# Loading eight channel tiles of x and of their weights singly instead of four, with the squares and the table product issued behind a later step

## The chip, the cores and the metric

The kernel runs on one core of a Trainium2 chip. The metric is the time of one execution on the device in microseconds (us), as the median of some runs. The engines named below are TensorE (PE, matmuls; PEld is its weight load), VectorE (DVE), ScalarE (ACT), GpSimd (POOL) and SyncE (SP, which here only issues DMAs).

## What is computed

One layer of a streaming encoder on 320 positions (256 of a prompt and 64 of a running stream), model width 2048, in float32. Cut to what matters:

```python
z = rmsnorm(x, ln_mix_g) @ w_in                # (320, 2048) @ (2048, 3328)
q, k, v, zs = split(z)                         # 1024, 128, 128, 2048 columns
bias = rel_bias_table[t5_bucket(q_pos - k_pos)]  # 16 heads, one table of 32 rows
a = sink_attention(rmsnorm(q), rmsnorm(k), v, bias, sinks)
s = u * (W_s @ rmsnorm(v_s) + b)               # u, v_s = halves of gelu(zs)
x = x + concat(rmsnorm(a), rmsnorm(s)) @ w_out
x = x + square(relu(rmsnorm(x) @ w_ffn_up)) @ w_ffn_down
```

## The kernel before

Everything is kept transposed: a tile has 128 channels on the partitions and the 320 positions along its rows. x is 16 such channel tiles (k = 0 to 15). A product runs over the channel tiles; for each block of weights of 256 output columns, PE adds up two banks of 128 columns. Float32 is brought to PE as two halves: the high half is the value rounded by an ACT copy (line 125 for weights, line 178 for x, where the gain is multiplied in), the low half is the rest, by DVE (lines 126 and 179). Three matmuls of 128x128 by 320 make one product: high by high, low x by high weight, high x by low weight (line 136).

The first product (`products` with `first=load_x`) is special: x itself is loaded in it, and two jobs go side by side, the k and v columns (tile `acc`) and the first 256 query columns (tile `q_ps`). `chunks` cuts the 16 channel tiles into steps: before, four steps of one tile and then three of four tiles. For each step `load_x` loads x and splits it, then for each of the two jobs the weights are loaded (`w_first`), split into `w_hi` and `w_lo` (three buffers each), and multiplied. So one tile brings 12 matmuls, and a step of four tiles 24 for each job. The norm of x is applied behind the product: squares of x (line 247, eight ACT instructions of two tiles each) are added up, and the reciprocal root is multiplied into the result.

The order of the instructions on each engine is laid out by a planner at build time, which takes the instruction that is ready first in its own reckoning, and among ready ones the one that comes earlier in the program. It can be held: `keep_in_program_order` puts an instruction behind the one before it on its engine in the program, which is done for the splits of the steps of one tile; `issue_after(ins)` puts what is in its block behind `ins` on the engine of `ins`. `steps` keeps, for each step and job, the ACT split, the DVE split and the last matmul: before, `steps[8]` and `steps[9]` are the two jobs of tiles 4 to 7.

The table product (line 228) multiplies the bias table by a one-hot matrix. Its result goes to `b_row` by a DVE copy (line 230), to `b_dram` in DRAM by a DMA of POOL (line 232), and from there by 16 loads into `bias`. These loads wait in the list `between`, and `load` (line 99) puts four of them behind each of the next loads of weights. All loads go out from SP in the one order in which `load` is called. The weights that come next, behind the first product, are those of the queries (`w_raw`, steps of four tiles).

Of the kernel before, what the change touches and what calls it, by code (L numbers as in the profile page):

```python
# [29 lines left out]
def hymba_step_kernel(ctx: ExitStack, tc: tile.TileContext, i, o):  # L30
# [13 lines left out]
    def misc():  # L44
        return ps_m.tile([P, 512], F32, name="misc", tag="misc")

    def big(name):
        return actp.tile([P, KT, T], F32R, name=name, tag="A", bufs=2)

    def blk(name, shape, dt=F32):  # L50
        return actp.tile(shape, dt, name=name, tag="B", bufs=6)
# [3 lines left out]
    xT = const.tile([P, KT, T], F32, name="xT")  # L55
    cols = const.tile([P, 58], F32, name="cols")
    g_mix, g_ffn = cols[:, 0:16], cols[:, 16:32]
# [34 lines left out]
    loads, between, steps = [], [], []  # L92

    def load(out, in_):


        for o_, i_ in [(out, in_)] + [between.pop(0) for _ in range(min(4, len(between)))]:
            with tc.issue_after(loads[-1].ins) if loads else nullcontext():
                loads.append(nc.sync.dma_start(out=o_, in_=i_))  # L99

    def chunks(n, first):
        if first:
            return [(a, 1) for a in range(4)] + [(a, 4) for a in range(4, n, 4)]
        return [(a, 4) for a in range(0, n, 4)]

    def products(w, k0, nk, jobs, rh, rl, first=None, deep=None):


        wv = w.rearrange("(kt p) n -> p kt n", p=P)
        steps.clear()  # L110
        for a, n in chunks(nk, first is not None):
            if first is not None:
                first(a, n)
                if a % 4 == 0:
                    ahead = blk("w_first", [P, len(jobs), 4, 256])
            for j, (c0, ps) in enumerate(jobs):
                if first is not None:
                    raw = ahead[:, j, a % 4:a % 4 + n]
                else:
                    raw = (deep or wp).tile([P, 4, 256], F32, name="w_raw", tag="w_raw")  # L120
                hi = wp.tile([P, 4, 256], F32R, name="w_hi", tag="w_hi", bufs=3)
                lo = wp.tile([P, 4, 256], F32R, name="w_lo", tag="w_lo", bufs=3)
                load(raw[:, :n], wv[:, k0 + a:k0 + a + n, c0:c0 + 256])
                pin = tc.keep_in_program_order if first is not None and a < 4 else lambda ins: ins
                high = pin(nc.scalar.activation(out=hi[:, :n], in_=raw[:, :n], func=AF.Copy))  # L125
                low = pin(nc.vector.tensor_tensor(out=lo[:, :n], in0=raw[:, :n], in1=hi[:, :n].bitcast(F32),  # L126
                                                  op=ALU.subtract))
                tail = isinstance(ps, list) and a + n == nk
                kgs = [(k, g) for g in range(2) for k in range(n)] if tail else [(k, g) for k in range(n) for g in range(2)]
                passes = [(w_, r_, x) for x, (w_, r_) in enumerate(((hi, rh), (hi, rl), (lo, rh)))]  # L130

                for (k, g), (w_, r_, x) in [(kg, p_) for p_ in passes for kg in kgs] if first is not None else \
                        [(kg, p_) for kg in kgs for p_ in passes]:
                    kk = a + k
                    out = ps[g][:, 0:T] if isinstance(ps, list) else ps[:, g, 0:T]
                    mm = nc.tensor.matmul(out=out, lhsT=w_[:, k, g * P:(g + 1) * P], rhs=r_(kk),  # L136
                                          start=(kk == 0 and x == 0), stop=(kk == nk - 1 and x == 2))
                steps.append((high.ins, low.ins, mm.ins))
# [10 lines left out]
    def product(w, k0, nk, c0, rh, rl, deep=None, apart=False):  # L149
        ps = [misc(), misc()] if apart else acc_tile()  # L150
        products(w, k0, nk, [(c0, ps)], rh, rl, deep=deep)
        return ps
# [22 lines left out]
    def split(src, g, hi, lo, pinned=False):  # L175

        pin = tc.keep_in_program_order if pinned else lambda ins: ins
        pin(nc.scalar.activation(out=hi, in_=src, func=AF.Copy, scale=g))  # L178
        pin(nc.vector.scalar_tensor_tensor(out=lo, in0=src, scalar=g, in1=hi.bitcast(F32), op0=ALU.mult,
                                           op1=ALU.subtract))  # L180


    XH, XL = big("XH"), big("XL")
    def load_x(a, n):
        load(xT[:, a:a + n], xv[:, a:a + n])
        for k in range(a, a + n):
            split(xT[:, k], g_mix[:, k:k + 1], XH[:, k], XL[:, k], pinned=a < 4)
    xh, xl = (lambda k: XH[:, k]), (lambda k: XL[:, k])
    w_in = i["w_in"]

# [3 lines left out]
    kv_ps = acc_tile()  # L194
    q0_ps = ps_sc.tile([P, 2, 512], F32, name="q0_ps", tag="s_ps")
    products(w_in, 0, KT, [(1024, kv_ps), (0, q0_ps)], xh, xl, first=load_x)

    kvx = blk("kvx", [P, 1152])
# [25 lines left out]


    b_ps = misc()
    with tc.issue_after(steps[9][2]):
        nc.tensor.matmul(out=b_ps[0:16, 0:255], lhsT=tab, rhs=oneh, start=True, stop=True)
    b_row = sm.tile([16, 255], F32, name="b_row", tag="w1", bufs=3)
    nc.vector.tensor_copy(out=b_row, in_=b_ps[0:16, 0:255])  # L230
# [12 lines left out]
    ssq2 = sm.tile([P, 2, T], F32, name="ssq2", tag="w2", bufs=4)  # L243
    for k in range(0, KT, 2):
        sq = sm.tile([P, 2, T], F32, name="sq2", tag="w2", bufs=4) if k else ssq2
        with tc.issue_after(steps[9][0]):
            nc.scalar.activation(out=sq, in_=xT[:, k:k + 2], func=AF.Square)
        if k:
            nc.vector.tensor_tensor(out=ssq2, in0=ssq2, in1=sq, op=ALU.add)
# [321 lines left out]
```

## Time and profile before

| | |
|---|---|
| median of 3 runs | 1263.6 us (1261.91 to 1265.82) |
| profiled execution | 1262.26 us |
| its span in the profile | 1259.7 us |
| PE busy | 1252.3 us, 8519 matmul records |
| DVE, ACT, POOL busy | 637.9, 489.4, 106.1 us |
| read from HBM | 182.91 MB |

The span is what the profile covers of one execution; the rest of the profiled execution's time lies around it. A timeline row gives the start, the busy time, engine, line, the tile written and those read, the shape, the count of merged instructions, and in brackets the idle time of the engine before it with what ended it. A matmul's record is longer than its share of the pace, since matmuls overlap. A row of an engine's queue (SPq) is the issue of a DMA, not its transfer.

### The profile page before, as it was taken

How to read it: one execution, taken by the hardware profiler on the slowest of the kernel's cores; microseconds unless marked ns; L12 is line 12 of the kernel's file. 1: busy time of each engine (PE TensorE's matmuls, PEld its weight loads, DVE VectorE, ACT ScalarE, POOL GpSimd, SP SyncE). 2: the span in 40 equal slices, each digit the busy share in tenths (PEclk: the TensorE clock that was granted, in tenths of full speed). 3: DMA queues.
4: the chain of work that ended last, by engine and by line, in shares of the span. 5: the costliest groups of instructions: out<-in, count | busy, mean ns of one | idle time of the engine just before them, and what ended most of it. 6: DMA issues, size and time to landing. Idle time of an engine off the chain costs nothing.

```text
span 1259.7 us, 20182 instructions
## 1 busy us (share of the span) xinstructions
PE 1252.3 (99%) x8519; PEld 1236.6 (98%) x8519; DVE 637.9 (51%) x731; ACT 489.4 (39%) x636; POOL 106.1 (8%) x104
## 2 busy tenths in 40 slices
PE   8999999999999999999999999999999999999998
PEld 7998889999999999999999999999999999999998
DVE  7547857756864444444444444444444334444443
ACT  7335546533543342223333333343333333343221
POOL 2213452400310000000000000000000000000000
PEclk9999999999999999999999999999999999999999
DMA  8643233644454444445544444455444444444550
GB/s 281 191 136 116 85 109 119 216 148 137 151 149 148 152 149 149 149 147 150 150 150 151 150 151 151 151 151 151 150 151 150 146 148 149 148 153 160 169 169 32
DMA packets 186426, 187.77 MB, mean 149 GB/s; under 512 B 6464, under 2 KB 185856, under 8 KB 186336
## 3 DMA queue, kind: packets, MB, share of 16 engines
q1 hardware_dynamic: 185696, 185.43, 47.2%
q8 instruction: 66, 1.08, 0.4%
q0 software_dynamic: 496, 1.03, 0.3%
q14 instruction: 24, 0.20, 0.0%
q10 hardware_dynamic: 144, 0.03, 0.0%
HBM read 182.91 MB, written 3.32 MB: 148 GB/s over the span
## 4 chain that ended last, share of the span: by engine, by line
PE 98%; DMA 0%; SPq 0%; ACT 0%; issue 0%; DVE 0%
PE acc L136 93%; PE misc L136 1%; PE q_ps L136 1%; PE s_ps L329 1%; PE misc L374 1%; PE misc L365 1%; DMA xT<-in_xT 0%; SPq L99 0%; PE misc L275 0%; PE misc L430 0%; PE misc L158 0%; PE misc L422 0%; PE misc L169 0%; ACT XH L178 0%; PE misc L431 0%; ACT w_hi L125 0%
## 5 line engine op out<-in xcount | busy, mean ns | idle before, releaser
L126 DVE TENSOR_TENSOR w_lo<-w_raw,w_hi 128x1024 fp32r<-128x1024 f32 x332 | 413.6, 1246 | 460.6 <-ACT w_hi L125 451.2
L125 ACT ACTIVATE w_hi<-w_raw 128x1024 fp32r<-128x1024 f32 x332 | 351.9, 1060 | 708.0 <-PE acc L136 674.6
L136 PE MATMUL acc<-H2H,w_hi 128*128 128x320 f32 x1024 | 316.6, 309 | 0.0
L136 PE MATMUL acc<-H2L,w_hi 128*128 128x320 f32 x1024 | 316.4, 309 | 0.0
L136 PE MATMUL acc<-H2H,w_lo 128*128 128x320 f32 x1024 | 316.4, 309 | 0.0
L136 PE MATMUL acc<-FH,w_hi 128*128 128x320 f32 x992 | 306.5, 309 | 0.0
L136 PE MATMUL acc<-FL,w_hi 128*128 128x320 f32 x992 | 306.5, 309 | 0.0
L136 PE MATMUL acc<-FH,w_lo 128*128 128x320 f32 x992 | 306.5, 309 | 0.0
L136 PEld LDWEIGHTS acc<-H2L,w_hi 128*128 128x128 f32 x1024 | 192.2, 188 | 0.0
L136 PEld LDWEIGHTS acc<-H2H,w_hi 128*128 128x128 f32 x1024 | 192.2, 188 | 0.0
L136 PEld LDWEIGHTS acc<-H2H,w_lo 128*128 128x128 f32 x1024 | 192.2, 188 | 0.0
L136 PEld LDWEIGHTS acc<-FH,w_hi 128*128 128x128 f32 x992 | 186.2, 188 | 0.0
L136 PEld LDWEIGHTS acc<-FL,w_hi 128*128 128x128 f32 x992 | 186.2, 188 | 0.0
L136 PEld LDWEIGHTS acc<-FH,w_lo 128*128 128x128 f32 x992 | 186.2, 188 | 0.0
L136 PE MATMUL acc<-XH,w_hi 128*128 128x320 f32 x384 | 117.2, 316 | 1.2 <-ACT w_hi L125 1.1
L136 PE MATMUL acc<-XH,w_lo 128*128 128x320 f32 x384 | 116.8, 315 | 0.0
L136 PE MATMUL acc<-XL,w_hi 128*128 128x320 f32 x384 | 116.6, 314 | 0.0
L136 PEld LDWEIGHTS acc<-XH,w_hi 128*128 128x128 f32 x384 | 71.2, 189 | 4.7 <-ACT w_hi L125 2.2
L136 PEld LDWEIGHTS acc<-XL,w_hi 128*128 128x128 f32 x384 | 71.4, 189 | 2.4 <-issue 1.9
L136 PEld LDWEIGHTS acc<-XH,w_lo 128*128 128x128 f32 x384 | 71.1, 188 | 2.2 <-issue 1.5
L488 DVE SCALAR_TENSOR_TENSOR tf<-acc,r 128x640 f32<-128x640 f32 x32 | 26.4, 825 | 42.7 <-PE acc L136 42.7
L502 DVE TENSOR_TENSOR xT<-xT,acc 128x640 f32<-128x640 f32 x31 | 25.5, 821 | 41.8 <-PE acc L136 41.8
(176 smaller groups left out, 1016.9 us busy)
## 6 DMA issues: line engine op xcount, KB each, us to landing
w_raw<-in_w_up SPq DMA_DIRECT2D x128, 512.0 KB
w_raw<-in_w_down SPq DMA_DIRECT2D x128, 512.0 KB
w_raw<-in_w_in SPq DMA_DIRECT2D x44, 512.0 KB
w_raw<-in_w_out SPq DMA_DIRECT2D x32, 512.0 KB
w_first<-in_w_in SPq DMA_DIRECT2D x6, 512.0 KB
out_yT<-xT SPq DMA_DIRECT2D x7, 320.0 KB
xT<-in_xT SPq DMA_DIRECT2D x3, 640.0 KB
w_first<-in_w_in SPq DMA_DIRECT2D x8, 128.0 KB
```

The costliest lines, as they stand in the source:

```text
L125: high = pin(nc.scalar.activation(out=hi[:, :n], in_=raw[:, :n], func=AF.Copy))
L126: low = pin(nc.vector.tensor_tensor(out=lo[:, :n], in0=raw[:, :n], in1=hi[:, :n].bitcast(F32), op=ALU.subtract))
L136: mm = nc.tensor.matmul(out=out, lhsT=w_[:, k, g * P:(g + 1) * P], rhs=r_(kk), start=(kk == 0 and x == 0), stop=(kk == nk - 1 and x == 2))
L329: nc.tensor.matmul(out=s_ps[:, j, 0:2 * nk].rearrange("x (p k) -> x p k", p=2), lhsT=qT[:, blk_, a:a + 2].rearrange("p a t -> p (a t)"), r ...
L365: nc.tensor.transpose(out=pt_ps[0:n, (2 * p + j) * P:(2 * p + j + 1) * P], in_=s[:, p, j, c:c + n], identity=ident)
L374: nc.tensor.matmul(out=o_ps[p * HD:(p + 1) * HD, 0:256], lhsT=v[0:n, kv], rhs=pt[0:n, p * 256:(p + 1) * 256], start=(x == 0), stop=(x == l ...
L488: nc.vector.scalar_tensor_tensor(out=t, in0=ps[:, :, 0:T], scalar=0.0, in1=r2[:, None, :].to_broadcast([P, 2, T]), op0=ALU.max, op1=ALU.mult)
L502: nc.vector.tensor_tensor(out=xT[:, a:a + n], in0=xT[:, a:a + n], in1=p, op=ALU.add)
```

## The change

In the first product the channel tiles 0 to 7, instead of 0 to 3, make steps of one tile each; tiles 8 to 15 stay two steps of four. The splits of x and of the weights are held in program order for all eight. With ten steps and two jobs, `steps` has 20 entries: 0 to 15 are the single tiles, 16 and 17 the two jobs of tiles 8 to 11. The table product now follows `steps[17]`, the last matmul of the second job of tiles 8 to 11; the squares follow `steps[11]`, the ACT split of the second job of tile 5.

```diff
     def chunks(n, first):
         if first:
-            return [(a, 1) for a in range(4)] + [(a, 4) for a in range(4, n, 4)]
+            return [(a, 1) for a in range(8)] + [(a, 4) for a in range(8, n, 4)]
...
-                pin = tc.keep_in_program_order if first is not None and a < 4 else lambda ins: ins
+                pin = tc.keep_in_program_order if first is not None and a < 8 else lambda ins: ins
...
-            split(xT[:, k], g_mix[:, k:k + 1], XH[:, k], XL[:, k], pinned=a < 4)
+            split(xT[:, k], g_mix[:, k:k + 1], XH[:, k], XL[:, k], pinned=a < 8)
...
-    with tc.issue_after(steps[9][2]):
+    with tc.issue_after(steps[17][2]):
         nc.tensor.matmul(out=b_ps[0:16, 0:255], lhsT=tab, rhs=oneh, start=True, stop=True)
...
-        with tc.issue_after(steps[9][0]):
+        with tc.issue_after(steps[11][0]):
             nc.scalar.activation(out=sq, in_=xT[:, k:k + 2], func=AF.Square)
```

## Rows read from the trace of the kernel before

**Rows 1.** From the page: the span, the first engine's busy time, the granted clock of PE in 40 slices, and the share of the engines in the chain that ended last.

```profile
span 1259.7 us, 20182 instructions
...
PE 1252.3 (99%) x8519; PEld 1236.6 (98%) x8519; DVE 637.9 (51%) x731; ACT 489.4 (39%) x636; POOL 106.1 (8%) x104
...
PEclk9999999999999999999999999999999999999999
...
PE 98%; DMA 0%; SPq 0%; ACT 0%; issue 0%; DVE 0%
```

**Rows 2.** All waits of PE in the whole span: who waited, for whom, us in total, how often, the longest.

```profile
PE q_ps L136 <- ACT w_hi L125: 1.5, 1, 1.5
PE misc L77 <- DVE hsel L87: 1.3, 1, 1.3
PE acc L136 <- ACT w_hi L125: 1.1, 1, 1.1
```

**Rows 3.** Two windows of the first product: the stretch, its length, the busy time of each engine in it, the granted clock, the busy share of the DMA engines and what they moved.

```profile
4.27:11.83 7.56, 7.50 (x42) 6.98 (x42) 4.53 (x11) 3.88 (x9) 2.97 (x7) 1.00 0.93 288
11.83:15.82 3.99, 1.33 (x9) 0.89 (x7) 2.30 (x6) 3.21 (x7) 0.00 (x0) 1.00 1.06 362
```

**Rows 4.** Timeline of PE over the first product.

```profile
13.51 0.56 PE L136 MATMUL q_ps<-XH,w_hi 128*128 128x320 f32 x2 [1.53 <-ACT w_hi L125]
...
15.82 1.44 PE L136 MATMUL acc<-XH,w_hi 128*128 128x320 f32 x8 [1.13 <-ACT w_hi L125]
...
23.05 0.60 PE L228 MATMUL misc<-oneh,tab 32*16 32x255 f32 x2
23.58 1.43 PE L136 MATMUL acc<-XH,w_hi 128*128 128x320 f32 x8
...
30.72 1.33 PE L136 MATMUL acc<-XH,w_hi 128*128 128x320 f32 x8
...
33.06 1.34 PE L136 MATMUL q_ps<-XH,w_hi 128*128 128x320 f32 x8
...
34.38 1.34 PE L136 MATMUL acc<-XH,w_lo 128*128 128x320 f32 x8
```

**Rows 5.** Timeline of ACT over the same stretch.

```profile
8.07 0.77 ACT L125 ACTIVATE w_hi<-w_first 128x256 fp32r<-128x256 f32 x2 [0.25 <-DMA w_first<-in_w_in]
...
12.59 0.56 ACT L178 ACTIVATE XH<-xT,cols 128x320 fp32r<-128x320 f32 x1 [2.91 <-DMA xT<-in_xT]
13.06 0.40 ACT L125 ACTIVATE w_hi<-w_first 128x256 fp32r<-128x256 f32 x1
...
14.73 2.12 ACT L125 ACTIVATE w_hi<-w_first 128x1024 fp32r<-128x1024 f32 x2
...
17.38 1.99 ACT L247 ACTIVATE sq<-xT 128x640 f32<-128x640 f32 x3
19.26 1.92 ACT L178 ACTIVATE XH<-xT,cols 128x320 fp32r<-128x320 f32 x4
```

**Rows 6.** Timeline of SP's queue: the issues of the loads.

```profile
3.56 0.43 SPq L99 DMA_DIRECT2D xT<-in_xT  x1
4.04 0.91 SPq L99 DMA_DIRECT2D w_first<-in_w_in  x2
...
6.41 0.43 SPq L99 DMA_DIRECT2D xT<-in_xT  x1
...
30.48 2.59 SPq L99 DMA_DIRECT2D bias<-b_dram  x4
33.12 0.44 SPq L99 DMA_DIRECT2D w_raw<-in_w_in  x1
```

**Rows 7.** Windows of 5 us (columns as in rows 3; the last one is GB/s).

```profile
0.00:5.00 5.00, 3.66 (x9) 2.58 (x10) 1.55 (x12) 2.35 (x4) 3.74 (x13) 1.00 0.55 141
5.00:10.00 5.00, 4.94 (x29) 4.54 (x29) 3.73 (x9) 3.88 (x9) 2.34 (x5) 1.00 0.90 272
10.00:15.00 5.00, 3.15 (x20) 2.61 (x18) 2.05 (x6) 2.41 (x6) 0.00 (x0) 1.00 1.03 345
```

**Rows 8.** The chain behind the table product: the copy and the DMA to DRAM in the timelines of DVE and POOL; and two lines of the list of DMA issues (KB of one, us from issue to landing).

```profile
24.31 0.40 DVE L230 COPY b_row<-misc 16x255 f32<-16x255 f32 x1
...
25.01 0.58 POOL L232 DMA_DIRECT2D b_dram<-b_row  x1 [17.52 <-DVE b_row L230]
...
b_dram<-b_row POOLq DMA_DIRECT2D x1, 239.1 KB, 5.5
...
out_kpT<-kvx POOLq DMA_DIRECT2D x1, 64.0 KB, 2.0
```

**Rows 9.** The second step (tiles 4 to 7) of the next product: its split on ACT and DVE, and its first matmul with the high half and its first with the low half in PE's timeline.

```profile
37.12 1.06 ACT L125 ACTIVATE w_hi<-w_raw 128x1024 fp32r<-128x1024 f32 x1 [5.33 <-DMA w_raw<-in_w_in]
...
38.21 1.23 DVE L126 TENSOR_TENSOR w_lo<-w_raw,w_hi 128x1024 fp32r<-128x1024 f32 x1 [4.50 <-ACT w_hi L125]
...
41.95 0.31 PE L136 MATMUL acc<-XH,w_hi 128*128 128x320 f32 x1
...
42.24 0.31 PE L136 MATMUL acc<-XH,w_lo 128*128 128x320 f32 x1
```

**Rows 10.** Two windows of 1 us, one of them while the table was written to DRAM (columns as in rows 3).

```profile
25.00:26.00 1.00, 1.00 (x9) 1.00 (x8) 1.00 (x2) 1.00 (x3) 0.58 (x1) 1.00 1.01 395
...
30.00:31.00 1.00, 1.00 (x9) 1.00 (x8) 1.00 (x3) 0.27 (x1) 0.00 (x0) 1.00 0.01 4
```

## The prediction

> **What bounds the kernel now.** I read the page first: TensorE (PE) is busy 1252.3 of 1259.7 us, its clock is granted in full in every slice, and the chain that ended last is PE for 98% [rows 1]. A microsecond in which PE stands still is therefore a microsecond of the result, and a microsecond saved on another engine is nothing unless PE was waiting for it. Next come PE's waits: there are three in the whole kernel, 1.5 and 1.1 us on line 136 for ACT's high half of the weights and 1.3 us before the warm-up [rows 2]. So all that can be won lies in the first 16 us. The windows by stage say where: from 4.27 to 11.83 PE is busy all but 0.06 us, from 11.83 to 15.82 only 1.33 us of 3.99 [rows 3]. The timeline shows what stood still: the second job of tile 3 starts at 13.51 instead of 11.83, and tiles 4 to 7 start at 15.82 [rows 4].
>
> ACT's timeline gives the reason [rows 5]. The high half for tile 3's second job (13.06) stands behind the split of x tile 4 (12.59), which waited 2.91 us for the transfer of x tiles 4 to 7, issued at 6.41 [rows 6]. Behind it come three more splits and the 1024-wide high half (14.73), and only then can PE go on. From 15.82 PE runs without a gap. Had it run on from 11.83 with tile 3's second job (12 matmuls of a tile go in 7.14/4 = 1.79 us, from the stretch 23.58 to 30.72 [rows 4], so half a tile is 0.89), tile 4 would have started at 12.72: the loss before tile 4 is 3.1 us, and that is the most that any cure of this gap can give.
>
> **Part 1: x and weights of tiles 4 to 7 one at a time.** PE work is unchanged (same matmuls, same order of tiles). Three transfers become twelve. SP issues a tile's three in 1.43 us (x at 3.56 for tile 2 and at 6.41 for tile 4, 2.85 for two tiles [rows 6]), so tile 7 is issued by 6.41 + 4 x 1.43 = 12.1 us; that is behind PE's back as long as the data come in time. A small transfer took 8.07 - 4.04 = 4.0 us from issue to use (tile 2's weights [rows 5, 6]); the 640 KB one took 12.59 - 6.41 = 6.2. With 4.5 for a small one in the loaded queue, tile 4 is there at 7.4 + 4.5 = 11.9 at the latest, then one tile each 1.43 us: 13.3, 14.7, 16.2. PE wants them at 12.72, 14.5, 16.3 and 18.1. ACT's part of a tile is one split and two 256-wide halves; by the pieces in a row (four splits 1.92 us, two such halves 0.77 [rows 5]) that is 0.48 + 0.77, 1.25 us, under PE's 1.79. So tiles 4 to 7 pass without a gap, and the twelve issues cost nothing, hidden behind PE's work on tiles 0 to 3. Without that cover each tile would cost 1.43 of SP instead of 1.79 of PE, still less.
>
> The queue shows 272 GB/s from 5 to 10 us, with mostly small transfers, and 345 GB/s from 10 to 15, with large ones [rows 7]. A tile is 416 KB, 426,000 bytes; in 1.79 us that is 238 GB/s, so the small ones suffice. The Trainium skill, "DMA: Bandwidth & Descriptors", section Rules for kernel authors, says the opposite of this change: at least 1 MiB in one DMA for full bandwidth. The table of its section Bandwidth gives 138 GB/s for 64 KB; by that a tile would take up to 3.1 us (an estimate from the page) and PE would starve. The row of 5 to 10 us speaks against so low a rate.
>
> **What is late next: tile 8.** x tiles 8 to 11 still come as one transfer, now issued at about 12.1; with the 6.2 us of its like it lands at 18.3. Four splits (1.92 us [rows 5]) and a 1024-wide high half (1.06, half of the 2.12 of two [rows 5]) follow: PE can start tile 8 at 21.3. It would be free for it at 19.9. Before, tiles 4 to 7 ended at 23.05. So the gain by then is at most 23.05 - 21.3 = 1.8 us of the 3.1; the other 1.4 reappear in front of tile 8.
>
> **Part 2: the squares.** They now stand behind the high half of tile 5's second job, at about 13.6. Four squares are 4 x 0.65 = 2.6 us (three took 1.99 [rows 5]); from 13.6 to 18.3 ACT has 2.5 us of work on tiles 6 and 7 and so 2.2 us to spare. Put in a block they delay tile 6 by some 0.6 us, which then runs up against the same 21.3. What costs more is a split of x tile 8 that the planner puts in front of a pinned high half, as it did with tile 4: in front of tile 7's second half the gain falls to 1.4, in front of tile 7's first to 1.0, in front of tile 6's second to 0.2 (each time ACT stands until 18.3 and the rest follows at the pace above). Split 8 is not pinned, so this can happen. I take a **gain of 1.5 us**, bounds 0.2 and 1.8. The remaining squares lie beside PE's work on tiles 8 to 15; ACT has 4 x 0.65 us left for them there, in the 14 us that PE takes for these tiles, so I see no price.
>
> **Part 3: the table product.** This is the part I think decides. The two matmuls (0.53 us, 23.05 to 23.58 [rows 4]) cost the same wherever they are. But they now stand behind tiles 8 to 11 instead of 4 to 7, that is 7.14 us later in PE's order. Their result feeds a chain: copy on DVE (24.31), a DMA from POOL to DRAM (25.01, 5.5 us to landing), then SP's loads of the bias, which read that DRAM and begin as it lands, at 30.48 [rows 6, 8]. And behind the first four bias loads stands, in SP's fixed order, the second weight block of the next product (33.12 [rows 6]), then four more and the third. ACT and DVE split that block at 37.12 and 38.21, done at 39.44; PE wants its low half at 42.24, its high one at 41.95 [rows 9]. The cover is 42.24 - 39.44 = 2.8 us.
>
> Let G be the gain and L the landing time of the DRAM write. The table product starts at 23.05 - G + 7.14 = 30.19 - G. With the same 1.96 us to POOL's issue (25.01 - 23.05), the bias loads begin at 32.15 - G + L, and the low half is done 39.44 - 30.48 = 8.96 us later, at 41.11 - G + L. PE wants it at 42.24 - G. G drops out: **PE waits L - 1.13 us**. With L = 5.5 as measured that is 4.4 us. But then the 16 DMA engines were full (25 to 26 us: share 1.01), and by 30 to 31 they are empty (0.01) [rows 10]; the lower bound is the 2.0 us of the 64 KB write to out_kpT [rows 8], which gives 0.9. L has 239 KB to carry, out of a queue that is empty; I take 3.5, nearer to the empty case: a **wait of 2.4 us**. The third block follows the second on SP by the time of four bias loads and one weight load (30.48 to 33.12 and 0.44, 3.1 us), and PE takes 3.5 us for a block, so there is one wait, not two. POOL's later work stands behind the DMA issue, which is now at about 30.7; its next instruction in the profile before, the clearing of a corner of the gating weights, has no reader in this product.
>
> **The sum.** -1.5 + 2.4 = +0.9 us; bounds -1.8 + 0.9 = -0.9 and -0.2 + 4.4 = +4.2. The profiled execution took 1262.26 us with a span of 1259.7; it becomes 1263.2. The median of the three runs, 1263.6, lies 1.3 above that execution, so the predicted median is 1264.5, no change. A measurement of this kernel tells a change from none at about 0.3%, 3.8 us.
>
> **The rivals.**
> (a) The table product slips further. It is of lower rank for the planner than the matmuls of tiles 12 to 15. It goes right behind tiles 8 to 11 only if PE is planned as idle there; in the kernel before it did sit right behind the matmul that it had to follow (23.05), and tile 12's low pass came after the other job's high one (34.38 behind 33.06 [rows 4]), so PE was planned as waiting for its operands there as well. If it is planned as busy, the product follows tile 15, another 7.14 us later: wait 9.5, sum +8.0, 1271.6. It decides from 2.8 us of delay on, microsecond for microsecond. Chance 0.13; this is the slower case.
> (b) The wait does not come, because the write lands near 2 us and the copy is quicker: sum -1.5 + 0.3, 1262.4. For it speak the empty DMA engines; against it that even 2.0 us leave 0.9. Chance 0.13.
> (c) The gap only moves to tile 7 or 8, G near 0.2, and the table's wait comes on top: +2.2, 1265.8. For it speaks that x split 4 was put in front of a half it should have followed. Chance 0.16.
> (d) Small transfers starve PE: at the 141 GB/s of the first 5 us [rows 7] a tile takes 3.0 us, tile 7 is 4 x (3.0 - 1.43) = 6.3 us later than above, and PE ends it at about 24.3 instead of 19.9, so that tile 8 starts there, 1.2 us later than before (23.05): sum 1.2 + 2.4 = +3.6, 1267.2. This is what the rule of the Trainium skill's page amounts to here. Against it stands the 272 GB/s row, and that the first 5 us are the filling of the queue. Chance 0.05.
> The forecast itself has 0.53.
>
> **How the numbers follow.** Faster by over 0.3% would need more than the 3.1 us that the gap holds: 0.02, measurement alone. Slower: (a) 0.13, half of (d), and the upper bound of the forecast and of (c) with 0.04, 0.2 in all. The rest, 0.78, is within 0.3%. The range 1261.5 to 1268.0 holds the forecast with its bounds (1262.7 to 1267.8), (b), (c) and (d); it leaves out (a) and a little at either end.
>
> **What would show it.** In the profile after: the gap of 1.5 us on tile 3's second job gone, PE waiting up to 1.4 us before tile 8 at about 21 us; the table product at about 28.7, SP's first bias load at about 34.2 and the next weights at 36.8; one new PE wait of 1 to 4 us on ACT or DVE at about 41 to 43 us. If the table product stands behind tile 15, (a) is right; if PE has no wait near 41 us, (b). The prediction is wrong if PE shows new waits later than 50 us, for which I see no cause.

## The result, and the profile after

The changed kernel takes 1270.61 us (median of 5 runs, 1267.14 to 1271.69) beside 1263.6 of 5 runs of the kernel before; the ratio is 1.0045, 95% interval [1.0033, 1.0057]. It is slower by more than 0.3%, and the prediction, no change at 1264.5 with 1268.0 as the upper end, was wrong. A second series gave 1270.95 and 1.0056 [1.0043, 1.0069].

The profiled execution took 1271.69 us. Its span is 10.2 us longer than that of the profile before [rows 1]. From the page: the span, the busy times, and the clock granted to PE in 40 slices.

```profile
span 1269.9 us, 20217 instructions
...
PE 1259.0 (99%) x8519; PEld 1242.3 (98%) x8519; DVE 638.8 (50%) x737; ACT 490.3 (39%) x642; POOL 105.1 (8%) x104
...
PEclk8899999999999999999999999999999999999999
```

Two things differ. PE is busy 6.7 us longer with the same 8519 matmuls, and two slices of the clock row, of 32 us each, show an 8 where all 40 showed a 9. PE was not only waiting more; it was working more slowly. PE's waits, answering to rows 2 (us in total, how often, the longest):

```profile
PE acc L136 <- ACT w_hi L125: 5.0, 3, 2.4
PE misc L77 <- DVE hsel L87: 1.3, 1, 1.3
PE q_ps L136 <- ACT w_hi L125: 1.3, 1, 1.3
```

All but the warm-up's are for the high half of weights: three with the result in `acc` (0.85 and 1.73 in the first product, 2.38 in the second) and one of 1.29 with `q_ps`, 6.3 us together, where there were 2.7. PE's timeline, answering to rows 4 and 9, shows where they lie:

```profile
12.67 0.46 PE L136 MATMUL acc<-XH,w_hi 128*128 128x320 f32 x2
...
17.20 0.56 PE L136 MATMUL acc<-XH,w_hi 128*128 128x320 f32 x2 [0.85 <-ACT w_hi L125]
...
21.12 0.56 PE L136 MATMUL acc<-XH,w_hi 128*128 128x320 f32 x2 [1.73 <-ACT w_hi L125]
...
23.59 0.90 PE L136 MATMUL q_ps<-XH,w_hi 128*128 128x320 f32 x2 [1.29 <-ACT w_hi L125]
...
25.36 2.33 PE L136 MATMUL acc<-XH,w_hi 128*128 128x320 f32 x8
...
34.50 0.60 PE L228 MATMUL misc<-oneh,tab 32*16 32x255 f32 x2
...
36.30 1.33 PE L136 MATMUL acc<-XL,w_hi 128*128 128x320 f32 x8
...
49.52 0.42 PE L136 MATMUL acc<-XH,w_hi 128*128 128x320 f32 x1 [2.38 <-ACT w_hi L125]
```

Tile 4 starts at 12.67 instead of 15.82: the old gap is cured. But tile 6 waits 0.85, tile 7 1.73 in its first job and 1.29 in its second, and PE is done with tile 7 and starts tile 8 at 25.36, while it was done with it at 23.05 before. The eight matmuls at 25.36 have a record of 2.33 us, eight of the same shape at 36.30 one of 1.33: little over half the pace. The windows (stretch, length, busy time of PE, PEld, DVE, ACT, POOL, granted clock, DMA share, GB/s) put the clock beside it:

```profile
4.28:16.36 12.08, 12.02 (x72) 11.09 (x72) 8.65 (x20) 9.19 (x21) 2.95 (x7) 1.00 0.91 285
16.36:23.59 7.23, 3.37 (x19) 2.65 (x19) 5.90 (x13) 5.41 (x13) 0.00 (x0) 0.96 1.02 333
23.59:30.10 6.51, 6.51 (x25) 6.51 (x26) 6.16 (x10) 6.17 (x10) 0.00 (x0) 0.52 0.98 333
30.10:34.50 4.40, 4.40 (x31) 4.21 (x29) 3.02 (x3) 1.89 (x2) 0.52 (x1) 1.00 0.05 18
47.10:49.52 2.42, 0.04 (x2) 0.01 (x1) 2.14 (x5) 1.11 (x2) 0.64 (x2) 1.00 0.74 198
50.50:57.10 6.60, 6.60 (x29) 6.60 (x29) 1.82 (x5) 2.52 (x3) 3.46 (x3) 0.50 0.84 253
```

Twice PE stood still for part of a stretch (3.9 of 7.23 us, then all of 2.42), and both times some 6.5 us of gapless work at a granted clock near 0.5, 1.2 GHz instead of 2.4, followed.

**The sum.** Tile 7 is done 2.3 us late. Of this 0.9 is half clock (the last 6 matmuls of tile 7, 23.59 to 25.36, took 1.77 instead of 6 x 0.149 = 0.89, with the pace of a matmul from the prediction's 7.14 us for 48), so 1.4 are waits, with the slower starts behind them. The 54 matmuls from 23.59 to 34.50, these 6 among them, took 10.9 us instead of 54 x 0.149 = 8.0: 2.9 by the clock. The wait at 49.52 adds 2.4. From there to 58.14 come 24 matmuls of 320 columns, 6 of line 158 and 10 of line 275; they took 8.6 us, and at full clock about 5.1 (24 at 0.147, the pace from 42.76 to 46.21; 0.58 for the 6; about 1.0 for the 10, by the half of 2.1 here): 3.5 by the clock. 1.4 + 2.9 + 2.4 + 3.5 = 10.2, the whole difference of the spans: 3.8 of waits and 6.4 of clock.

**Who held PE in front.** ACT's timeline, answering to rows 5:

```profile
14.24 0.72 ACT L247 ACTIVATE ssq<-xT 128x640 f32<-128x640 f32 x1
14.87 1.98 ACT L247 ACTIVATE sq<-xT 128x640 f32<-128x640 f32 x3
16.75 0.71 ACT L125 ACTIVATE w_hi<-w_first 128x256 fp32r<-128x256 f32 x2
...
19.74 1.01 ACT L178 ACTIVATE XH<-xT,cols 128x320 fp32r<-128x320 f32 x2 [1.82 <-DMA xT<-in_xT]
20.66 0.40 ACT L125 ACTIVATE w_hi<-w_first 128x256 fp32r<-128x256 f32 x1
20.97 1.00 ACT L178 ACTIVATE XH<-xT,cols 128x320 fp32r<-128x320 f32 x2
21.88 1.35 ACT L247 ACTIVATE sq<-xT 128x640 f32<-128x640 f32 x2
23.13 2.30 ACT L125 ACTIVATE w_hi<-w_first 128x256 fp32r<-128x256 f32 x3
```

Four squares (14.24 to 16.75) stand in front of tile 6's high halves, and PE waits 0.85. Then the splits of x tiles 8 and 9 stand in front of tile 7's first half and wait for their transfer (1.82 us, to 19.74), and the splits of tiles 10 and 11 and two more squares stand in front of its second half (23.13).

**Who held PE at 49.5.** SP's queue, answering to rows 6, ACT's timeline, and from the list of DMAs the landing of the table's write:

```profile
41.13 3.26 SPq L99 DMA_DIRECT2D bias<-b_dram  x4
44.43 0.44 SPq L99 DMA_DIRECT2D w_raw<-in_w_in  x1
```

```profile
48.41 1.06 ACT L125 ACTIVATE w_hi<-w_raw 128x1024 fp32r<-128x1024 f32 x1 [13.91 <-DMA w_raw<-in_w_in]
```

```profile
b_dram<-b_row POOLq DMA_DIRECT2D x1, 239.1 KB, 4.2
```

The chain is the predicted one, 6 to 8 us later than predicted, since the front is late and tiles 8 to 11 ran in part at half clock: table product 34.50, bias loads 41.13, weights 44.43, their high half 48.41, PE 49.52.

### The profile page after: what moved, and what is told of

Same layout as the page of the kernel before. It is cut to its first block, busy times and chain, and to the rows that moved or that the text cites. A ratio compares the mean times of both kernels' runs of the same rounds, so it can differ in the third digit from the quotient of the medians.

```text
span 1269.9 us, 20217 instructions
## 1 busy us (share of the span) xinstructions
PE 1259.0 (99%) x8519; PEld 1242.3 (98%) x8519; DVE 638.8 (50%) x737; ACT 490.3 (39%) x642; POOL 105.1 (8%) x104
## 4 chain that ended last, share of the span: by engine, by line
PE 97%; DMA 2%; SPq 1%; ACT 0%; DVE 0%; issue 0%; ACTq 0%; DVEq 0%
PE acc L136 92%; PE misc L136 1%; PE s_ps L329 1%; SPq L99 1%; PE misc L374 1%; PE misc L365 1%; DMA xT<-in_xT 1%; PE q_ps L136 0%; PE misc L275 0%; DMA b_dram<-b_row 0%; DMA w_first<-in_w_in 0%; DMA w_raw<-in_w_in 0%; PE misc L430 0%; PE misc L158 0%; PE misc L422 0%
## 5 line engine op out<-in xcount | busy, mean ns | idle before, releaser
L136 PE MATMUL acc<-XH,w_hi 128*128 128x320 f32 x384 | 119.9, 322 | 5.0 <-ACT w_hi L125 5.0
```

## The experiments

Each kernel was timed beside the kernel before on the same chip; the ratio is to that, with its 95% interval. The theory after the first profile had three parts: the table product's place delays the weights behind the bias loads; the squares and the unheld splits delay tiles 6 and 7; and PE's clock follows its standstills. The rivals were that small transfers starve PE, and that the wait at 49.5 has to do with something else than SP's order.

**The table product back behind tiles 4 to 7**, the rest as changed:

```diff
-    with tc.issue_after(steps[17][2]):
+    with tc.issue_after(steps[15][2]):
```

> The changed kernel with the table product alone put back behind tile 7 (steps[15], the place it had in channel tiles). Theory A (three separate costs: ACT's order in front of tiles 6 to 8; the late table product; the clock that fell to half after each of the two stalls): the PE wait of 2.4 us at 49.5 us and the half clock from 50.6 to 57.4 us are gone, the gaps of 0.9, 1.7 and 1.3 us before 24 us and the half clock from 23.3 us stay; about 5 us less than the changed kernel's profiled run, 1266. Theory B (the small transfers are the cause, the table product only follows the late start): no more than 1 us less, and a wait near 49 us stays.

1264.19 us, 0.9999 [0.999, 1.0008], which is 6.4 us under the changed kernel. No wait near 49 us, and full clock from 44 to 56 us. The front is as in the changed kernel, gaps of 0.85, 1.49 and 1.29 and then half clock:

```profile
22.00:24.00 2.00, 1.08 (x4) 1.08 (x5) 1.89 (x4) 2.00 (x4) 0.00 (x0) 0.52 1.08 353
24.00:26.00 2.00, 2.00 (x7) 0.84 (x6) 1.32 (x3) 2.00 (x4) 0.00 (x0) 0.50 1.10 372
26.00:28.00 2.00, 2.00 (x8) 2.00 (x9) 2.00 (x4) 2.00 (x5) 0.58 (x1) 0.50 1.04 381
```

So the table's place, with the clock that hangs on it, carries nearly all of the median's 7 us. That the front's gaps and their half clock cost nothing against the kernel before fits the mean clocks at the end of the next section: most runs of the kernel before lose a stretch of clock too.

**The table product late, nothing else** (in the kernel before):

```diff
-    with tc.issue_after(steps[9][2]):
+    with tc.issue_after(steps[11][2]):
```

> The kernel before with the table product alone moved behind tiles 8 to 11 (steps[11] there). Theory A: PE waits near 42 us by the landing time of the DRAM write less 1.1 us, with the 4.2 us now measured some 3 us, and if the clock then falls as in the changed kernel another 3 us: 1266.5 to 1269.5 against 1263.6. Theory B: the load order alone does nothing, 1263.6, within 1 us.

1267.28 us, 1.0021 [1.0011, 1.0031]: 2.65 over the kernel before. In its profile the write lands in 4.2 us again, and PE waits 0.88 for the high and 0.70 for the low half of the second block at 48 to 49 us, 1.6 us where some 3 were expected, without losing the clock there. The mechanism works alone, at a smaller price. The front, which is that of the kernel before, waited 3.49 and 1.14 us in this profile (1.53 and 1.13 in [rows 4]) and ran at half clock behind it (0.50 from 18 to 22 us): the same instructions do not always wait as long.

**Splits held up to tile 11**, the rest as changed:

```diff
-            split(xT[:, k], g_mix[:, k:k + 1], XH[:, k], XL[:, k], pinned=a < 8)
+            split(xT[:, k], g_mix[:, k:k + 1], XH[:, k], XL[:, k], pinned=a < 12)
```

> The changed kernel with the splits of x tiles 8 to 11 held in program order too, squares and table product as in the change. Theory A: the wait of 1.7 us in front of tile 7's first job goes; a square of tiles 8 and 9 now stands in front of tile 7's second high half in ACT's order and waits for the same transfer (landed at 19.7), so a gap of about 2 us in front of that job stays; the 0.9 us in front of tile 6 (four squares) stays. About 1 us less than the changed kernel, 1269.5. Theory B: no change.

1270.03 us, 1.0035 [1.0025, 1.0046]: 0.6 less than the changed kernel, no more, and inside the intervals. Gaps of 0.85, 1.15 and 1.62 stay in front (the squares still stand there), as does one of 2.02 at 47.5, and both half-clock stretches. The hoisted splits alone were not the trouble here.

**All three together**: table product after `steps[15][2]`, squares after `steps[17][0]`, splits held up to tile 11.

> The changed kernel's eight single tiles kept, with splits of tiles 8 to 11 held in order, squares behind the first high half of tiles 8 to 11, table product behind tile 7. Theory A: PE runs from tile 0 to the end of tile 7 without a gap (end at about 19.5 us), waits 1 to 2 us for tile 8 (x lands at 19.7), no wait near 49 us and no half clock after that; 1.5 us under the kernel before, 1262. Theory B: gaps stay in front of tiles 5 to 7 with the weights' or x's transfer as the releaser, over 1265.

1261.3 us, 0.9973 [0.9963, 0.9984]: faster than the kernel before. PE runs from tile 0 to tile 7 without a gap (tile 7 ends at 19.6), and the only wait in the product is that for x tiles 8 to 11. Its row in PE's timeline, and ACT's:

```profile
22.06 1.47 PE L136 MATMUL acc<-XH,w_hi 128*128 128x320 f32 x8 [1.83 <-ACT w_hi L125]
```

```profile
19.14 1.92 ACT L178 ACTIVATE XH<-xT,cols 128x320 fp32r<-128x320 f32 x4 [1.91 <-DMA xT<-in_xT]
```

This is the prediction's own picture of tile 8: landed 19.1 (18.3 predicted), PE 22.06 (21.3). Behind this one wait, too, the clock was 0.50 from 24 to 26 us.

**Two of the three.** Table product back and squares late, splits not held:

> The changed kernel with the table product behind tile 7 and the squares behind the first high half of tiles 8 to 11; splits of tiles 8 to 11 not held. Theory A: the gap of 0.9 us in front of tile 6 is gone, ACT reaches the split of tile 8 sooner but still waits there for x until about 19.5 us, in front of both high halves of tile 7: one gap of 2 to 2.5 us in front of tile 7, under 1 us in front of tile 8; 1262 to 1263, 1 to 2 us less than with the table product alone (1264.2). If the squares were not the cause of the gap in front of tile 6: 1264.

1262.47 us, 0.9988 [0.9979, 0.9997], the time as expected, with one gap of 1.25 and one of 0.3 us where 2 to 2.5 were. Table product back and splits held, squares as changed:

> The changed kernel with the table product behind tile 7 and the splits of tiles 8 to 11 held in order; squares as in the change. Theory A: gaps as in the run with the splits alone held (0.9 in front of tile 6, 1.2 inside tile 7, 1.6 in front of tile 8), no wait near 49 us; 1263.5 to 1264.5, no better than the table product alone (1264.2), since a square of tiles 8 and 9 takes the split's place in front of tile 7's second high half.

1262.03 us, 0.9982 [0.9973, 0.9991]: a miss, better than I expected. In its profile there are gaps of 0.85 and 0.81 only, and its mean clock was 1.000 in 9 of 10 runs. So with the table product back either cure of the front gives about 2 us (1264.19 less 1262.47 or 1262.03) and both together 2.9. Only the last of these differences is clear of the intervals ([0.9963, 0.9984] against [0.999, 1.0008] with the table product alone). Why the held splits bring 2.2 us here and only 0.6 beside the late table is not settled; the clock that one kernel keeps and the other loses twice is the visible difference. The two pairs ran on two chips, on which the kernel before took 1264.63 and 1264.67.

**The table late, but the bias loads out of the way.** To tell SP's order from any other effect of the late table, the 16 loads were queued behind the first blocks of weights of the third product; the table product stays as late as in the change:

```diff
-                between.append((bias[hh * HD:(hh + 1) * HD, p, j], src))
...
+        if g == 2:
...
+                        between.append((bias[hh * HD:(hh + 1) * HD, p, j], src))
```

> The changed kernel as it is, the table product as late as in the change, but the 16 bias loads put into SP's order behind the first weight blocks of the third product instead of the second. Theory A (PE waited near 49.5 us because the weights stood behind the bias loads on SP, and these behind the DRAM write): no wait of PE on w_raw and no half clock after 45 us, the gaps before 24 us unchanged; as fast as with the table product put back (1264.2 measured), 1263.5 to 1265. Rival (the late table product costs by itself, through the norm or the engines it occupies): 1268 or more.

1263.35 us, 0.9993 [0.9984, 1.0001]: 7.3 under the changed kernel, with no wait on `w_raw`. SP's queue shows the weights ahead of the bias:

```profile
33.11 4.61 SPq L99 DMA_DIRECT2D w_raw<-in_w_in  x2
38.92 3.08 SPq L99 DMA_DIRECT2D bias<-b_dram  x4
```

The late table itself costs nothing; what costs is what stands behind its readers in SP's queue. The front's gaps stay (0.85, 0.62 and 1.28), and half clock behind them (0.50 from 22 to 25 us).

**PE kept busy in the wait.** The changed kernel with 14 matmuls by a tile of zeros between the first and the second step of the second product, which add nothing to the result:

```diff
+    zero = const.tile([P, P], F32R, name="zero")
...
+                if fill and not steps:
+                    for _ in range(fill.pop()):
+                        mm = nc.tensor.matmul(out=out, lhsT=zero, rhs=rh(0), start=False, stop=False)
```

> The changed kernel with 14 matmuls by a tile of zeros (2.05 us at full clock, added to the sum that is open) put between the first and the second step of the second product, where PE waits 2.4 us in the changed kernel. They do no useful work and end before the awaited weights. Theory A (the clock fell because PE stood still there): the first matmul of tiles 4 to 7 starts at the same time as in the changed kernel, but the granted clock stays at full from 45 to 60 us; about 3 us less than the changed kernel, 1267.5. Rival (the clock falls there whatever PE does, or because of the short matmuls of the norms behind the wait): half clock as before, no gain, 1270 to 1271.

1267.85 us, 1.0026 [1.0018, 1.0034]: 2.8 faster than the changed kernel, by more work (its interval just touches that of the changed kernel's first series and is clear of the second's). In its profile PE still waits 0.55 and 0.71 us for the weights, behind the filler, and the clock stays full:

```profile
43.66 1.86 PE L144 MATMUL acc<-XH,zero 128*128 128x320 f32 x11
...
46.07 0.41 PE L140 MATMUL acc<-XH,w_hi 128*128 128x320 f32 x1 [0.55 <-ACT w_hi L129]
```

Half of its 12 runs had a mean clock of 1.000 and 5 one of 0.997, while none of the changed kernel's ten had 1.000 and six had 0.996 or less. The weights came no sooner: they were issued 10.0 us behind the table product (30.78 to 40.82), 9.9 in the changed kernel. What the filler saves is the clock.

**The kernel before with its splits held**, to see whether the hoisted split of tile 4 was the cost that the change set out from:

```diff
-            split(xT[:, k], g_mix[:, k:k + 1], XH[:, k], XL[:, k], pinned=a < 4)
+            split(xT[:, k], g_mix[:, k:k + 1], XH[:, k], XL[:, k], pinned=a < 8)
```

> The kernel before, steps of four from tile 4 on, with the splits of x tiles 4 to 7 alone held in program order. If the split in front of a high half was the whole cause of the gap in the kernel before: 1.5 us or more less, 1262.5 to 1263 against 1264.6. If the step of four is (its transfer lands at 12.6 us and four splits and a wide half follow): tile 3 is done without a gap, but tile 4 starts at 15.5 to 15.8 us as before, one gap of nearly 3 us in place of two; no gain, 1264 to 1265, and the clock falls to half behind it at least as often.

1264.42 us, 1.0002 [0.9993, 1.0011]. The two gaps become one, in front of tile 4:

```profile
16.24 2.50 PE L136 MATMUL acc<-XH,w_hi 128*128 128x320 f32 x8 [3.57 <-ACT w_hi L125]
```

The large transfer costs PE some 3 us there in either order. In the kernels run here the gap in front of tile 4 went only with the smaller ones.

**All sixteen tiles one at a time**, all splits held, the squares spread one by one, the table product after `steps[15][2]`:

```diff
-            return [(a, 1) for a in range(8)] + [(a, 4) for a in range(8, n, 4)]
+            return [(a, 1) for a in range(n)]
...
-        with tc.issue_after(steps[11][0]):
+        with tc.issue_after(steps[min(31, 2 * k + 13)][0]):
```

> All sixteen tiles in steps of one, all splits held in order, each square behind the second high half of a tile six later, table product behind tile 7. Theory A: no transfer of four tiles is left that an ACT instruction in order can stand behind, ACT needs 1.25 us for a tile and 0.33 for its share of the squares against 1.79 of PE: PE runs from 4.3 us through the product without a gap over 0.5 us, full clock in all runs, 1.8 us less than the version with eight (1261.3), 1259 to 1260. Theory B (many small transfers starve PE): gaps with a transfer as releaser between tiles 8 and 15, 1262 or more.

1266.12 us, 1.0013 [1.0004, 1.0023]: a miss by 6 us, though PE has no gap at all in the first product. The wait stands behind it, for the first weights of the second, and the clock is lost there:

```profile
37.97 0.64 PE L136 MATMUL acc<-XH,w_hi 128*128 128x320 f32 x1 [3.51 <-ACT w_hi L125]
```

```profile
27.32 0.43 SPq L219 DMA_DIRECT2D sgb<-in_sgu_b  x1
...
28.27 0.43 SPq L99 DMA_DIRECT2D w_raw<-in_w_in  x1
```

```profile
38.00:44.00 6.00, 5.64 (x21) 5.24 (x22) 4.39 (x5) 2.66 (x3) 0.00 (x0) 0.53 0.70 209
```

Two loads of 512 KB for a later stage (`sgb`, `wsT`) stand in front of those weights, and SP, which now issues 48 small transfers, reaches them at 28.27.

**The same with the queue cleared**: `sgb`, `wsT` and the 16 bias loads moved behind the weights of the second product.

> The version with sixteen single tiles, and on SP the two loads for the gating (512 KB each) and the 16 bias loads moved behind the weight blocks of the second product. If the 3.5 us that PE waited there in the version with sixteen came from what stood before the weights in the queue: that wait is under 0.5 us, PE has no other wait after 4.3 us, the clock is full in all or nearly all runs (no standstill, no half clock), 1258.5 to 1260 against 1264.3 for the kernel before. If the weights themselves come too late for a product that runs without gaps (the queue is at its rate): a wait of 2 us or more stays at 35 to 38 us, often with half clock behind it, 1262 to 1265.

1259.94 us, 0.997 [0.996, 0.998], better than both kernels. Mean clock 1.000 in all 9 runs, which lie between 1259.70 and 1260.96. One wait is left, in the first block of the second product, 1.04 us where under 0.5 was expected, and SP's order shows why it is no longer:

```profile
PE acc L136 <- DVE w_lo L126: 1.0, 1, 1.0
```

```profile
27.41 8.84 SPq L99 DMA_DIRECT2D w_raw<-in_w_in  x4
36.30 0.50 SPq L295 DMA_DIRECT2D sgb<-in_sgu_b  x1
```

**The changed kernel once more**, for a second profile:

> The changed kernel once more, for the granted clock of more runs: 1269 to 1272, most runs with a mean clock of 0.994 to 0.997 (one or two stretches at half clock), the runs with the highest clock the fastest; a run at 1.000 would come to 1265.5 to 1266.5.

1270.95 us (above). This time the front kept its clock, with gaps of 0.84, 1.33 and 1.28, and the table product came at 31.57, 2.9 us earlier than in the first profile; but the wait is 4.55 us, with 9.25 us of half clock behind it:

```profile
48.75 0.63 PE L136 MATMUL acc<-XH,w_hi 128*128 128x320 f32 x1 [4.55 <-ACT w_hi L125]
```

```profile
44.00:48.70 4.70, 0.20 (x3) 0.06 (x1) 2.11 (x4) 1.06 (x2) 1.16 (x2) 0.93 0.77 215
48.75:58.00 9.25, 9.25 (x38) 9.25 (x39) 3.90 (x5) 3.57 (x5) 3.47 (x3) 0.50 0.82 253
```

The weights did not follow the earlier table product, because on DVE the copy of its result stands behind a low half that belongs to the next product, and that one waited for weights that SP had issued at 24.16, no sooner than in the first profile (24.13):

```profile
34.11 1.23 DVE L126 TENSOR_TENSOR w_lo<-w_raw,w_hi 128x1024 fp32r<-128x1024 f32 x1 [1.03 <-ACT w_hi L125]
35.26 0.48 DVE L251 TENSOR_TENSOR ssq<-ssq 128x320 f32<-128x320 f32 x1
35.66 0.41 DVE L230 COPY b_row<-misc 16x255 f32<-16x255 f32 x1
```

From table product to copy it took 4.1 us here, 1.7 in the first profile (34.50 to 36.21), 1.3 before [rows 4, 8].

## Why the prediction was wrong

**Part 1 was right.** Tile 4 starts at 12.67 (12.72 predicted), and SP's twelve issues cost nothing. Rival (d), starved PE, is refuted: 285 GB/s flowed from 4.28 to 16.36, and in the kernel with all tiles single PE ran its whole first product without a gap. The Trainium skill, "DMA: Bandwidth & Descriptors", section Rules for kernel authors, asks for at least 1 MiB in one DMA for full bandwidth. The trace agrees that larger transfers bring more at a time (333 GB/s from 16.36 to 23.59 beside these 285), but the time went the other way: the versions with transfers far under that size and the other waits taken away took 1261.3 and 1259.94 us against 1264.

**The gain had the wrong sign:** 1.4 us lost by waits where 1.5 were to be won. The first step that failed is "Put in a block they delay tile 6 by some 0.6 us, which then runs up against the same 21.3", and behind it the price list for one hoisted split. The block's delay was well sized (0.85). But I priced squares and splits as cases for themselves, and the list had one split in front of one half; in fact two splits stood in front of each half of tile 7, with two squares more, and the transfer came at 19.7 instead of 18.3 (issued at 12.46, 7.3 us, not 6.2). ACT's 2.2 us to spare were spent twice. That this is the cause is shown by taking away both (1261.3 against 1264.19, with the table product back in place, and no gap left in front of tiles 6 and 7); taking away either goes the same way (1262.47, 1262.03).

**Part 3 was right in mechanism and about right in size.** The wait on the second block was 2.38 us in one profile and 4.55 in the other; 2.4 was forecast, with 0.9 and 4.4 as bounds. The landing took 4.2 and 4.3 us, not 3.5, which by L - 1.13 makes 3.1 to 3.2, between the two. That the first profile's 2.38 meets the 2.4 is in part chance: POOL's issue came 0.45 us later and the landing took 0.7 longer, but PE came to the block 0.6 later behind the table product (12.64 us, not 12.05), and the high half, for which it waited, was there 0.6 sooner behind the first bias load (8.39 us) than the 8.96 that the prediction took for the low half. What the formula had wrong is "the same 1.96 us to POOL's issue": POOL issued 2.4 us behind the table product in the first profile and 4.8 (31.57 to 36.36) in the second, since DVE does a low half for the next product first. So G does not drop out: a front that is quicker by 2.9 us brought the weights only 0.5 us earlier (bias loads at 40.63 instead of 41.13), and the rest came back as wait. Moving the bias loads removed it (1263.35). Rival (a) was false: the product came right behind tiles 8 to 11. So was (b). Rival (c), the gap moved and the table's wait on top, 1265.8, is what happened, still 5 us short; that (a)'s 1271.6 lies near the result is chance.

**The second step that failed, and the dearer one, is the clock**, the largest term of the difference: 6.4 of 10.2 us. I read "its clock is granted in full in every slice" from one execution and worked with it as with a constant: "A microsecond in which PE stands still is therefore a microsecond of the result" puts the clock at nothing. In this kernel a wait in which PE stands still can be followed by half clock: 2.38 us of wait were followed by 3.5 of loss, 3.9 us in three gaps by 2.9. The filler, which only kept PE busy, gave 2.8 us back; that is the direct test. The Trainium skill, "TensorE: Matmul & The Clock Gate", section HAM oscillation — how this bites in real kernels, tells of matmuls that start at the lower clock behind a wait for a DMA, and of keeping PE at work as the cure. The rows agree with it (0.52 and 0.50 behind the waits, full clock behind the filled one), but not for every wait: behind 0.88 and 0.70 us, with only the table late, the clock stayed full.

**The sign that I passed over** was the 1.3 us between the profiled run of the kernel before and the median. I carried them over as an offset. Of 93 runs of the kernel before, taken beside these experiments, 11 had a mean clock of 1.000 (median 1262.1 us), 25 one of 0.999 (1263.9), 4 of 0.998 (1263.1) and 53 of 0.997 (1264.9). The profile I read (1262.26 us, 1.000) was like the 11; most runs of the kernel before lose a stretch of clock themselves (0.997 is also the mean clock of the profile with the table product back, with 7 us of half clock at its front). This is also why the medians differ by 7.0 us and the two profiled runs by 9.4.

## What to carry to other kernels

Price a standstill of the engine that bounds the kernel at its length and, where its clock can fall behind it, at more, and look at the mean clock of several runs before taking "full clock" from one profile. When a step is moved later, follow its readers into the queues with a fixed order: what stands behind them there (here weights behind bias loads) pays, and moving those readers back did here what moving the step back does (1263.35 and 1264.19). When an engine has slack, spend it once: write out the order of its instructions with all moves made, not one move at a time, and hold the early instructions of a later step that could be put in front of a needed one.

## What was not expected of the hardware

- PE's granted clock fell to 1.2 GHz not only after one long standstill: after 0.85, 1.73 and 1.29 us with work between them it was 0.52 from 23.59 to 30.10. With gaps of nearly the same size (0.84, 1.33, 1.28) it stayed full in another run of the same kernel, and behind smaller ones (0.85, 0.62, 1.28, with the bias loads moved) it fell again. What decides between them is open. The changed kernel's runs differ by 4.6 and 4.1 us in its two series, those of the best version, whose one wait is of 1.04 us, by 1.3 over 9 runs; those of the kernel before by 5.1 over 21 on one chip.
- The write of 239 KB to DRAM took 4.2 and 4.3 us with nothing else in the queue (a DMA share of 0.00 from 34.50 to 38.00), against 5.5 in the full one. The write itself then filled the engines (shares of 1.27 and 0.97 from 38 to 40 us, at 133 and 97 GB/s; 0.75 to 0.86 from 37 to 40 in the second profile). An empty queue was no reason to take this write at little more than half its time.
